# MLA queries as 12 packed tiles with rotary rows placed by DMA and the query norm in the softmax; first loads on a second queue, b heads folded after the transpose, a shorter last token tile

## The chip, the cores and the metric

The kernel runs on one core of a Trainium2 chip. The metric is the device time of one execution in microseconds, and lower is better. The engines are named as in the profile: PE is the matrix engine (TensorE) and PEld its loading of weights, DVE the vector engine, ACT the scalar engine, POOL the GpSimd engine and SP the engine that issues most transfers; SPq and ACTq are the queues of SP and ACT for transfers. All transfers run on the core's 16 DMA engines.

## The reference

Two layers of a streaming encoder are run for a prompt of 256 frames and for eight sample streams of 16 new frames each, which gives 384 columns in all. Layer 0 holds a banded attention ("a", 8 heads) and a differential attention ("b", 4 heads of two maps), layer 1 a multi-head latent attention (MLA, 16 heads). Each mixer stands between two SwiGLU feed-forward blocks, and a final RMSNorm ends the program. What the change touches is this:

```python
def c_project(h, pos, w_in, g_q, g_kv, w_q_up):          # MLA, projections
    cq, ckv, kr = split(h @ w_in, [384, 640])
    q = (rmsnorm(cq, g_q) @ w_q_up).reshape(b, s, 16, 64 + 32)
    q_nope, q_rope = q[..., :64], rope(q[..., 64:], pos)
    ckv = rmsnorm(ckv, g_kv)
    kr = rope(kr, pos)                                    # one rotary key for all heads
def c_attend(q_nope, q_rope, k_nope, v, k_rope, ...):     # MLA, attention
    logits = (q_nope . k_nope + q_rope . k_rope) * 96 ** -0.5
    p = masked_softmax(logits, mask); return p @ v
def rope(x, pos):                                         # x1, x2: the two halves of the 32
    return concat([x1 * cos - x2 * sin, x1 * sin + x2 * cos])
def b_attend(...):                                        # b heads: two maps, one difference
    p = masked_softmax(logits, mask)
    w = p[map 0] - lam * p[map 1]; return w @ v
y = rmsnorm(y, final_norm)                                # the end
```

## The kernel before

**Products.** Activations stand with features on the partitions and the 384 frames along the free axis. Every projection in full precision is made of three products of reduced operands (`mm3`, through `mm`, L94): a weight is split into a high part wh (cast on ACT, L102) and a low part wl (subtraction on DVE, L103), an activation into its own two parts, and high*high, high*low and low*high are summed in PSUM. `load_w` (L105 to L114) issues the transfer of one weight tile `raw` from SP (L109) and makes wh and wl; there are three buffers of each. Small products in plain fp32 (attention, transposes against the identity, column sums) take two passes in the array and show as two records each.

**Order.** The code names the work in one order; the order in which the instructions stand on each engine is set by a scheduling pass over the whole program. An engine runs its own list strictly in that order, and waits where an operand or a buffer isn't there yet. SP's list is the queue of transfers: one that waits holds up all behind it.

**MLA query projection.** `mla_mixer` makes three tiles cq (384 features), two tiles ckv and the rotary key kr; o_ckr (L740) writes kr out, and three ACT copies (L742) repeat its 32 rows down the 128 partitions of kr4. Then the loop over c = 0 to 7 loads one tile of q_up and makes two 128x384 output tiles of nine products each, so 16 tiles and 144 products. A head takes one whole tile of 128 rows: 64 nope rows, 32 rotary rows and the same 32 rows with their halves swapped; the 64 rotary rows meet cos and sin in the tables te and to, and `query` (L776) multiplies each tile by its table, which also carries the query's norm. That norm is brought from columns to all rows by `spread` (L164: three diagonal tiles dg, multiplied by ones). The results are qq: qh for even heads, ql for odd heads. POOL copies the sample columns of the rotary rows to qrs (L778).

**MLA keys.** ke and ko hold the keys of even and odd heads: one half of the partitions from the product of wk and ckv (L807, L808), the other half filled with kr4 by one broadcast transfer each (L798, L799; 64 rows of 8 x 256). The sample queries are multiplied into the latent space by 32 products of wkT and qh or ql (even heads on partitions 0 to 63, odd heads on 64 to 127), which fill qa. Then scores over the cached latents (tiles cb, L853), softmax and values follow, woven with the prompt heads (`soft_prompt`, L372: bias, scale and minimum in one DVE pass; exp on ACT, L374).

**b heads, sample side.** For each of 8 streams the 128 rows of exp hold 4 heads x 2 maps x 16 frames. `turn` (L528) brings them to the key side through `comb_w`, an fp32 product that transposes and adds the two maps at once (L94, T<-comb_w,se); the a heads use a transpose instead (L535). ACT copies the result to pT (L538). `new` does the same for the new frames' weights pn. The PSUM tile T comes from a pool with one buffer, which the transposes of the prompt heads (L401) use too.

**Start and end.** SP issues the gains (L121), then the first eight halves of weights (L966) in turn with the eight tiles of x (L968); until they come, PE runs 14 products of ones. At the end `down_tokens` closes the last feed-forward block token tile by token tile: `half` squares a half on ACT (L279) and multiplies it by the final gains on DVE (L281), `finish` makes the norm from the two sums (L286 to L291) and scales and writes y in two parts (L293 to L296).

Of the kernel before, what the change touches and what calls it, by code (L numbers as in the profile page):

```python
# [11 lines left out]
F32 = mybir.dt.float32  # L12
# [28 lines left out]
C_ID, C_COMB, C_BM, C_M0, C_TE, C_TO = 0, 128, 192, 200, 202, 586  # L41
C_N = 970
# [24 lines left out]
def trunk(ctx, tc, I, O):  # L67
# [56 lines left out]
    comb = con[:, C_COMB:C_COMB + 64]  # L124
    bmask = con[:, C_BM:C_BM + NB]
    rope_e = con[:, C_TE:C_TE + N]
    rope_o = con[:, C_TO:C_TO + N]
# [122 lines left out]
    def down_tokens(fp, gt, down):  # L250
# [26 lines left out]
        def half(t, hf):  # L277
            sq = fp.tile([P, 512], F32, name="fq", bufs=2)
            nc.scalar.activation(sq, ps[t][hf], AF.Square, accum_out=sm[:, t, hf:hf + 1])  # L279
            sl = slice(hf * 512, hf * 512 + 512)  # L280
            nc.vector.tensor_tensor(out=ys[t][:, sl], in0=ps[t][hf], in1=gfin[:, sl], op=ALU.mult)  # L281

        def finish(t):
# [9 lines left out]
            nc.vector.tensor_scalar(y[:, 384:], y[:, 384:], rc, None, op0=ALU.mult)  # L293
            nc.sync.dma_start(out=O["y"][t * P:(t + 1) * P, 384:], in_=y[:, 384:])
            nc.scalar.activation(y[:, :384], y[:, :384], AF.Copy, scale=rc)  # L295
            nc.scalar.dma_start(out=O["y"][t * P:(t + 1) * P, :384], in_=y[:, :384])  # L296
# [69 lines left out]
    def soft_prompt(ap, S, bias, c, bufs=2):  # L366
# [4 lines left out]
        for j, sl, bsl in ((0, slice(0, 128), slice(128, 256)), (1, slice(128, 384), slice(0, 256))):  # L371
            nc.vector.tensor_tensor_reduce(out=s[:, sl], in0=S[:, sl], in1=bias[:, bsl], scale=-c, scalar=BIG,  # L372
# [57 lines left out]
    def even_mixer(sub, g_next):  # L430
        with ExitStack() as es:
# [6 lines left out]
            for nm, nh in (("b", 4), ("a", 8)):  # L438
# [8 lines left out]
            comb_w = mp.tile([P, P], F32, name="comb_w")  # L447
            nc.gpsimd.memset(comb_w, 0.0)
            nc.gpsimd.tensor_copy(out=comb_w.rearrange("p (h w) -> p h w", h=4)[:, :, :NT],
                                  in_=comb.rearrange("p (h t) -> p h t", h=4))  # L450
# [48 lines left out]
            def sample(nm, nout):  # L499
# [6 lines left out]
                rc = ident if nm == "a" else comb_w  # L506
# [22 lines left out]
                def turn(b, e):  # L529
# [4 lines left out]
                    if nm == "a":  # L534
                        nc.tensor.transpose(T[:, :P], e[:, :PAST], ident)  # L535
                    else:
                        mm(T[:, :P], e[:, :PAST], comb_w, True, True)
                    nc.scalar.copy(out=pT, in_=T[:, :P])  # L538
# [17 lines left out]
                def new(hf):  # L556

                    T = ps_t.tile([P, 512], F32, name="T")
                    mm(T[:, :P], pn.rearrange("p b t -> p (b t)"), rc, True, True)
                    pnT = ap.tile([P, P], F32, name="pnT", bufs=1)  # L560
                    nc.scalar.copy(out=pnT, in_=T[:, :P])
# [21 lines left out]
            def b_prompt():  # L583
                q, k, v, _ = qkv["b"]

                def weights(h, _):
                    S = scores_prompt(*[(q[r, h], k[r, h]) for r in (slice(0, 64), slice(64, 128))])
                    (e0, r0), (e1, r1) = [soft_prompt(ap, s, bt["b"][0][:, h], 1.0, 4) for s in S]
# [39 lines left out]
            def a_prompt():  # L628
# [4 lines left out]
                def weights(h, _):  # L633
                    i = h // 2
                    if h % 2 == 0:
                        S[h], S[h + 1] = scores_prompt(*[(q[r, i], k[r, i]) for r in (slice(0, 64), slice(64, 128))])
                    return normed(ap, *soft_prompt(ap, S[h], bt["a"][0][:, h], 1.0, 4))
# [51 lines left out]
    def mla_mixer(sub, g_next):  # L689
        with ExitStack() as es:  # L690
# [43 lines left out]
            nc.vector.tensor_tensor(out=kt, in0=rope_o[0:64], in1=rstd[0:64], op=ALU.mult)  # L734
# [4 lines left out]
            nc.vector.tensor_tensor(out=kr4[0:32], in0=kr4[0:32], in1=krs, op=ALU.add)  # L739
# [3 lines left out]
            nc.gpsimd.tensor_copy(out=kr4s[:, :, PAST:], in_=kr4[:, NP:].rearrange("p (b t) -> p b t", b=NB))  # L743
# [4 lines left out]
            te = slot([P, N], F32, "te", "oh5")  # L748
            to = slot([P, N], F32, "to", "ol5")
            ckl = lambda ct, sl: (cks[ct][0][:, sl], cks[ct][1][:, sl])  # L750

            def norms():

                rq = spread(rcq, 0)[:, :N]
                nc.vector.tensor_tensor(out=te, in0=rope_e, in1=rq, op=ALU.mult)
                nc.vector.tensor_tensor(out=to, in0=rope_o, in1=rq, op=ALU.mult)
# [16 lines left out]
            nc.gpsimd.memset(qrs, 0.0)  # L773

            def query(c, r, ps):
                nc.vector.tensor_tensor(out=qq[r][c], in0=ps[:, :N], in1=(te, to)[r], op=ALU.mult)  # L776
                rp = slice(64 * (1 - r), 64 * (1 - r) + 64)
                nc.gpsimd.tensor_copy(out=qrs[rp, r, :, c], in_=qq[r][c][rp, NP:].rearrange("p (b t) -> p b t", b=NB))  # L778

            held = []  # L780
            for c in range(8):
                w = load_w(I["q_up"][c], 768, cuts=2)
                for r in range(2):
                    ps = ring_tile()
                    for k in range(3):
                        mm3(ps[:, :N], blk(w, 3 * r + k), cqs[k], k == 0, k == 2)
                    held.append((c, r, ps))
                    if (c, r) in ((1, 0), (2, 0), (4, 0)):
                        next(nm)
                    if c:  # L790
                        for a in held:
                            query(*a)
                        held = []
# [56 lines left out]
            def scores():  # L850
                def weights(b, _):
# [14 lines left out]
                    nc.vector.tensor_scalar(mx, mx, -C_SCALE, None, op0=ALU.mult)  # L866
# [61 lines left out]
            def prompt():  # L928
                def weights(h, _):
                    i, r = h // 2, h % 2  # L930
                    S, = scores_prompt((qq[r][i], kk[r][:, i]))
                    return normed(ap, *soft_prompt(ap, S, bmsk, C_SCALE, 3))
# [158 lines left out]
```

## Time and profile before

| what | value |
|---|---|
| median of 3 runs | 1477.79 us (1477.79 to 1477.84) |
| the profiled execution | 1477.37 us, of which the span is 1475.6 us |
| PE busy | 1464.2 us, 99% of the span |
| DVE, ACT, POOL busy | 798.6, 598.3 and 82.6 us |
| granted clock, mean | 0.999 of full speed |
| PE busy in 1054.60 to 1082.50, the query projection | 27.72 of 27.90 us |
| PE busy in 1082.50 to 1102.00, keys and latent queries | 19.05 of 19.50 us |

The span is the time from the first to the last record of the trace; the 1.77 us around it belong to launch and end. A start time in a row is counted from the beginning of the span. Matmuls overlap in the array, so that the duration of a record (0.34 us) is longer than its share of time: the time that a product takes is read from the distance between two starts.

### The profile page before, as it was taken

Reading aid. Unit: us, or ns where it says so; the run is one execution under the profiler, and the core shown is the slowest. Engines: PE = TensorE matmul, PEld = TensorE weight load, DVE = VectorE, ACT = ScalarE, POOL = GpSimd, SP = SyncE. Lnnn points to the kernel's source line nnn. Section 1 sums busy time; section 2 is a strip of 40 time slices with the busy share of each in tenths; the row PEclk is TensorE's granted clock in tenths of the full one; section 3 lists DMA queues with packets and bytes.
Section 4 is the critical chain, followed back from the end, with each engine's and each line's share of the span. In section 5 each row is a group of like instructions: output and inputs, shape, how many; then the busy total and the mean of one; then the engine's idle time right before and its main releaser. Section 6 shows DMA issues by size and latency. Waiting matters only on the chain. (4 is left out here: it accounts for less than half of the span.)

```text
span 1475.6 us, 21816 instructions
## 1 busy us (share of the span) xinstructions
PE 1464.2 (99%) x8683; PEld 1399.7 (95%) x8683; DVE 798.6 (54%) x1456; ACT 598.3 (41%) x1036; POOL 82.6 (6%) x118
## 2 busy tenths in 40 slices
PE   9999999999999999999999999999999999999997
PEld 9999999998778999999999999999997999999886
DVE  7655543357486655553356555443867575555323
ACT  6433333335365433333334333333468453333323
POOL 2000001111001000000100000011110010000000
PEclk9999999999999999999999999999999999999999
DMA  7343344545442343434443333444541243333332
GB/s 242 129 129 127 123 122 119 174 154 169 157 161 97 129 129 129 129 122 118 132 129 128 123 125 125 120 131 143 172 129 44 67 137 128 129 127 124 121 123 78
DMA packets 72501, 191.66 MB, mean 130 GB/s; under 512 B 6704, under 2 KB 27216, under 8 KB 72016
## 3 DMA queue, kind: packets, MB, share of 16 engines
q1 hardware_dynamic: 71968, 189.69, 40.5%
q8 instruction: 68, 1.11, 0.3%
q10 hardware_dynamic: 432, 0.59, 0.1%
q14 instruction: 33, 0.27, 0.1%
HBM read 184.04 MB, written 5.16 MB: 128 GB/s over the span
## 5 line engine op out<-in xcount | busy, mean ns | idle before, releaser
L102 ACT CAST wh<-raw 128x1024 fp32r<-128x1024 f32 (+3 forms) x376 | 340.3, 917 | 762.9 <-issue 288.3
L103 DVE TENSOR_TENSOR wl<-raw,wh 128x1024 fp32r<-128x1024 f32 (+3 forms) x376 | 399.3, 1069 | 287.4 <-ACT wh L102 284.5
L94 PE MATMUL acc<-xh,wh 128*128 128x384 f32 x728 | 245.1, 337 | 0.0
L94 PE MATMUL acc<-xl,wh 128*128 128x384 f32 x728 | 243.4, 334 | 0.0
L94 PE MATMUL acc<-xh,wl 128*128 128x384 f32 x728 | 243.3, 334 | 0.0
L94 PE MATMUL S<-xl,wh 128*128 128x384 f32 x432 | 144.6, 335 | 0.7 <-DVE xl L222 0.7
L94 PE MATMUL S<-xh,wh 128*128 128x384 f32 x432 | 145.0, 336 | 0.0
L94 PE MATMUL S<-xh,wl 128*128 128x384 f32 x432 | 144.3, 334 | 0.0
L94 PEld LDWEIGHTS acc<-xh,wh 128*128 128x128 f32 x728 | 136.2, 187 | 2.5 <-issue 1.9
L94 PEld LDWEIGHTS acc<-xl,wh 128*128 128x128 f32 x728 | 136.3, 187 | 0.9 <-issue 0.2
L94 PEld LDWEIGHTS acc<-xh,wl 128*128 128x128 f32 x728 | 136.2, 187 | 0.3
L184 POOL TENSOR_TENSOR ssq<-ssq,sq 128x384 f32<-128x384 f32 x45 | 53.5, 1189 | 909.7 <-ACT sq L183 899.1
L94 PEld LDWEIGHTS S<-xl,wh 128*128 128x128 f32 x432 | 81.1, 188 | 2.0 <-DVE xl L222 1.7
L94 PEld LDWEIGHTS S<-xh,wh 128*128 128x128 f32 x432 | 81.1, 188 | 0.3
L94 PEld LDWEIGHTS S<-xh,wl 128*128 128x128 f32 x432 | 81.1, 188 | 0.0
L94 PE MATMUL acc<-gl,wh 128*128 128x384 f32 x220 | 74.3, 338 | 0.0
L94 PE MATMUL acc<-gh,wh 128*128 128x384 f32 x220 | 74.3, 338 | 0.0
L94 PE MATMUL acc<-gh,wl 128*128 128x384 f32 x220 | 74.3, 338 | 0.0
L94 PE MATMUL M<-xh,wh 128*128 128x384 f32 x216 | 72.2, 334 | 0.0
L94 PE MATMUL M<-xl,wh 128*128 128x384 f32 x216 | 72.2, 334 | 0.0
L94 PE MATMUL M<-xh,wl 128*128 128x384 f32 x216 | 72.1, 334 | 0.0
L94 PE MATMUL L<-xh,wh 128*128 128x384 f32 x208 | 69.5, 334 | 0.0
(434 smaller groups left out, 2672.9 us busy)
## 6 DMA issues: line engine op xcount, KB each, us to landing
raw<-gu SPq DMA_DIRECT2D x172, 512.0 KB, 3.3
raw<-dn SPq DMA_DIRECT2D x70, 512.0 KB, 3.5
raw<-dn SPq DMA_DIRECT2D x24, 384.0 KB, 3.2
raw<-e_in SPq DMA_DIRECT2D x16, 512.0 KB, 3.5
raw<-e_v SPq DMA_DIRECT2D x8, 512.0 KB, 4.0
raw<-e_out SPq DMA_DIRECT2D x8, 512.0 KB, 3.8
raw<-c_out SPq DMA_DIRECT2D x8, 512.0 KB, 3.3
raw<-q_up SPq DMA_DIRECT2D x8, 384.0 KB, 3.3
```

The source lines that it names most:

```text
L94: nc.tensor.matmul(out, lhsT=l, rhs=r, start=start, stop=stop)
L102: nc.scalar.copy(out=h, in_=src)
L103: (eng or nc.vector).tensor_tensor(out=l, in0=src, in1=h.bitcast(F32), op=ALU.subtract)
L184: nc.gpsimd.tensor_tensor(out=self.acc, in0=self.acc, in1=sq, op=ALU.add)
```

## The change

1. MLA queries. The 16 heads' 32 rotary rows are packed into four tiles of 128 rows, the 64 nope rows into eight: 12 tiles of nine products. The swap of halves moves to the key side: kr4 now holds, per 64 rows, the rotary key and its swapped copy, placed by five transfers instead of three ACT copies, and the cached keys come with swapped rows. The rotary tiles are multiplied by cos and by sin (`rotary`, into the tiles turned0 and turned1, which use the memory of ke and ko), and `place` carries them to their heads' rows in qq by 32 transfers of 32 x 384 numbers (48 KB) inside the core's memory. The nope tiles are copied to qq by ACT, 16 copies of 64 x 384. The query's norm isn't multiplied in any more: it goes as a scale per row into the softmax (ncq for the prompt, csq for the samples; csq comes from one product of 128 x 8), and `spread` stays for the keys alone.
2. b heads. comb_w is gone: the weights are transposed as for the a heads, and `both_maps` adds the two maps with two DVE operations, from PSUM to pT (ten times: eight streams and two halves of new frames). The a heads' two products for pn become transposes as well.
3. Start. The gains and the first two tiles of x are issued from ACT's queue.
4. End. The second half of the last token tile isn't multiplied by the gains by itself; one DVE operation multiplies it by gains and norm from PSUM. ACT comes first, and the two parts are cut at 512 instead of 384.

```diff
-    nc.sync.dma_start(out=gains, in_=I["gains"])
+    nc.scalar.dma_start(out=gains, in_=I["gains"])
...
-            nc.sync.dma_start(out=xd, in_=I["xT"][:, d])
+            (nc.scalar if d < 2 else nc.sync).dma_start(out=xd, in_=I["xT"][:, d])
...
-            nc.vector.tensor_tensor(out=ys[t][:, sl], in0=ps[t][hf], in1=gfin[:, sl], op=ALU.mult)
+            if t < TT - 1 or hf < HF - 1:
+                nc.vector.tensor_tensor(out=ys[t][:, sl], in0=ps[t][hf], in1=gfin[:, sl], op=ALU.mult)
...
+                nc.vector.scalar_tensor_tensor(y[:, cut:], ps[t][1], rc, gfin[:, cut:], op0=ALU.mult, op1=ALU.mult)
...
+            def both_maps(out, T):
+                m = [T[:, :P].rearrange("p (h m t) -> p h m t", h=4, m=2)[:, :, i:i + 1].to_broadcast([P, 4, 2, NT])
+                     for i in range(2)]
+                nc.vector.tensor_copy(out=out.rearrange("p (h m t) -> p h m t", h=4, m=2), in_=m[0])
+                nc.vector.tensor_tensor(out=out.rearrange("p (h m t) -> p h m t", h=4, m=2),
+                                        in0=out.rearrange("p (h m t) -> p h m t", h=4, m=2), in1=m[1], op=ALU.add)
...
-                        mm(T[:, :P], e[:, :PAST], comb_w, True, True)
-                    nc.scalar.copy(out=pT, in_=T[:, :P])
+                    nc.tensor.transpose(T[:, :P], e[:, :PAST], ident)
+                    settle(pT, T)
...
+            for at in (32, 96):
+                nc.sync.dma_start(out=kr4[at:at + 16], in_=kr4[16:32])
+                nc.sync.dma_start(out=kr4[at + 16:at + 32], in_=kr4[0:16])
+            nc.sync.dma_start(out=kr4[64:96], in_=kr4[0:32])
             nc.sync.dma_start(out=O["ckr"], in_=kr4[0:32])
-            for j in range(1, 4):
-                nc.scalar.copy(out=kr4[32 * j:32 * j + 32], in_=kr4[0:32])
...
+            def rotary(c, w):
+                for j in range(2):
+                    ps = up(w, j)
+                    for t, tab in enumerate((rcos, rsin)):
+                        nc.vector.tensor_tensor(out=turned[c][:, j, t], in0=ps[:, :N], in1=tab, op=ALU.mult)
+            def place(c):
+                for j in range(2):
+                    for q in range(4):
+                        h = 8 * c + 4 * j + q
+                        r = h % 2
+                        for t in range(2):
+                            at = 64 * (1 - r) + 32 * t
+                            nc.sync.dma_start(out=qq[r][h // 2][at:at + 32], in_=turned[c][32 * q:32 * q + 32, j, t])
+            w = load_w(I["q_rope"][0], 768, cuts=2)
+            w1 = load_w(I["q_rope"][1], 768, cuts=2)
+            rotary(0, w)
+            w = load_w(I["q_nope"][0], 768, cuts=2)
+            rotary(1, w1)
+            place(0)
+            next(nm)
+            for c in range(4):
+                w1 = load_w(I["q_nope"][c + 1], 768, cuts=2) if c < 3 else None
+                if c == 0:
+                    place(1)
+                for j in range(2):
+                    ps = up(w, j)
+                    for r in range(2):
+                        rr = slice(64 * r, 64 * r + 64)
+                        nc.scalar.copy(out=qq[r][2 * c + j][rr], in_=ps[rr, :N])
...
                     for r in range(2):
                         nc.scalar.activation(e[:, r], S[:, r * NK:(r + 1) * NK], AF.Exp, bias=mx[:, r:r + 1],
-                                             scale=C_SCALE, accum_out=sm[:, r:r + 1])
+                                             scale=csq[:, 0, b:b + 1], accum_out=sm[:, r:r + 1])
```

How the change moves instructions is shown at three places. The first is SP's queue in the query projection. Before, from the rotary key's write-out to the first loads for the output projection, it holds:

```order
L740 DMA o_ckr<-kr_9792 32x384
L799 DMA ko<-kr_9792 64x8x256
L109 DMA raw<-q_up 128x768 x2
L798 DMA ke<-kr_9792 64x8x256
L109 DMA raw<-q_up 128x768
L109 DMA raw<-wk 128x1024 x2
L766 DMA o_ckv<-ckv 128x2x384
L109 DMA raw<-c_out 128x1024 x6
```

After the change the same stretch holds 16 rows of placing (L812), two transfers each, of which the last three stand here:

```order
L753 DMA o_ckr<-kr_9800 32x384
L812 DMA qh_9832<-turned_9850 32x384 x2
...
L812 DMA ql_9846<-turned_9851 32x384 x2
L812 DMA qh_9839<-turned_9851 32x384 x2
L812 DMA ql_9847<-turned_9851 32x384 x2
L783 DMA o_ckv<-ckv 128x2x384
L109 DMA raw<-q_nope 128x768
L842 DMA ke<-kr_9800 64x8x256
L843 DMA ko<-kr_9800 64x8x256
L109 DMA raw<-wk 128x1024 x2
```

The fourth load of q_nope, the two key broadcasts and the loads of wk now stand behind 32 placings, with five transfers for kr4 ahead of o_ckr, and both broadcasts stand directly ahead of wk.

The second place is PE's list where the sample queries meet wkT. Before, even heads (qh) and odd heads (ql) alternate, after the value products, 31 of them in one row:

```order
L94 MATMUL acc<-wh,ckvl_9690 128x512
L94 MATMUL M<-ql_9831,wkT 128x128
L94 MATMUL S<-qh_9824,wkT 128x128
L94 MATMUL M<-ql_9832,wkT 128x128
L94 MATMUL S<-qh_9825,wkT 128x128
L94 MATMUL M<-ql_9833,wkT 128x128
```

After the change they stand in groups of one kind at three places: twelve ahead of the seventh nope tile, eight behind the last, twelve after the value products. The first group is this:

```order
L94 MATMUL S<-cqh_9688,wl 128x384
L94 MATMUL S<-qh_9832,wkT 128x128
L94 MATMUL S<-qh_9833,wkT 128x128
L94 MATMUL S<-qh_9834,wkT 128x128
L94 MATMUL S<-qh_9835,wkT 128x128
L94 MATMUL L<-qh_9836,wkT 128x128
L94 MATMUL L<-qh_9837,wkT 128x128
...
L94 MATMUL S<-ql_9844,wkT 128x128
L94 MATMUL S<-ql_9845,wkT 128x128
L94 MATMUL M<-cqh_9639,wh 128x384
```

Products of even and odd heads, which stood side by side in pairs, now mostly follow products of their own kind; the row M<-cqh begins the seventh nope tile, which needs the fourth load of q_nope.

The third place is PE's list in the b heads, where the turn of pn is followed by the next turn of se; both go into T, and the rows between are an input projection. Before:

```order
L94 MATMUL acc<-xh_1903,wh 128x384
L94 MATMUL T<-comb_w,pn 128x128
L94 MATMUL acc<-xl_1904,wh 128x384
L94 MATMUL acc<-xh_1903,wl 128x384
L94 MATMUL acc<-xh_1994,wh 128x384
L94 MATMUL T<-comb_w,se 128x128
```

After:

```order
L94 MATMUL acc<-xh_1903,wh 128x384
L566 MATMUL T<-con,pn 128x128
L94 MATMUL acc<-xl_1904,wh 128x384
L94 MATMUL acc<-xh_1903,wl 128x384
L94 MATMUL acc<-xh_1994,wh 128x384
L94 MATMUL acc<-xl_1995,wh 128x384
L94 MATMUL acc<-xh_1994,wl 128x384
L94 MATMUL acc<-xh_2087,wh 128x384
L544 MATMUL T<-con,se 128x128
```

Six products instead of three now lie between the two users of T.

## Rows read from the trace of the kernel before

**Rows 1.** page, part 1, TensorE: busy us (share) x instructions
```profile
PE 1464.2 (99%) x8683; PEld 1399.7 (95%) x8683; DVE 798.6 (54%) x1456; ACT 598.3 (41%) x1036; POOL 82.6 (6%) x118
```

**Rows 2.** timeline of PE, MLA query tiles: start us, us, engine, line, operation, output<-inputs
```profile
1054.60 0.42 PE L94 MATMUL L<-cqh,wh 128*128 128x384 f32 x1
...
1056.26 0.34 PE L94 MATMUL acc<-cqh,wh 128*128 128x384 f32 x1
...
1057.84 0.34 PE L94 MATMUL S<-cqh,wh 128*128 128x384 f32 x1
...
1059.95 0.34 PE L94 MATMUL M<-cqh,wh 128*128 128x384 f32 x1
...
1061.16 0.42 PE L94 MATMUL M<-cql,wh 128*128 128x384 f32 x1
...
1082.53 0.28 PE L94 MATMUL acc<-ckvh,wh 128*128 128x256 f32 x1
```

**Rows 3.** timeline of PE, the products with wkT, to the first cb
```profile
1097.95 0.37 PE L94 MATMUL M<-ql,wkT 64*128 64x128 f32 x1
...
1098.27 0.27 PE L94 MATMUL M<-ql,wkT 64*128 64x128 f32 x1
1098.28 0.27 PE L94 MATMUL S<-qh,wkT 64*128 64x128 f32 x1
...
1101.71 0.51 PE L94 MATMUL acc<-cb,qa 128*128 128x144 f32 x2
```

**Rows 4.** timeline of SP, the issuing of transfers: start us, us to issue
```profile
1.66 0.50 SPq L968 DMA_DIRECT2D x<-xT  x1
2.20 0.43 SPq L966 DMA_DIRECT2D raw<-gu  x1
...
1056.38 0.36 SPq L740 DMA_DIRECT2D o_ckr<-kr  x1
```

**Rows 5.** DMA issues of 1050 to 1090: count, KB each, median us to landing
```profile
raw<-q_up SPq DMA_DIRECT2D x5, 384.0 KB, 3.3
...
raw<-wk SPq DMA_DIRECT2D x2, 512.0 KB, 4.3
ko<-kr SPq DMA_DIRECT2D x1, 512.0 KB, 5.4
```

**Rows 6.** timeline of ACT, the cast of the second wk load
```profile
1079.43 1.05 ACT L102 CAST wh<-raw 128x1024 fp32r<-128x1024 f32 x1 [2.11 <-PE acc L94]
```

**Rows 7.** timeline of PE, a turn of b weights, then one of a
```profile
355.67 0.49 PE L94 MATMUL T<-comb_w,se 128*128 128x128 f32 x2
356.09 0.45 PE L94 MATMUL L<-kb,qbd_b 128*32 128x144 f32 x8
...
424.48 0.33 PE L535 MATMUL T<-con,se 128*128 128x128 f32 x1 [0.33 <-ACT wT L403]
424.74 0.45 PE L94 MATMUL L<-kb,qbd_a 128*32 128x144 f32 x8
```

**Rows 8.** instructions on tile pT, 340 to 385: ns min/median/max
```profile
L538 ACT COPY pT<-T x6: 239/258/266, 348.8 to 384.0; 128x128 f32<-128x128 f32 x6
```

**Rows 9.** timeline of DVE, one pass over 128x128 numbers
```profile
353.04 0.28 DVE L526 TENSOR_SCALAR se<-se,ssm 128x128 f32<-128x128 f32 x1
```

**Rows 10.** waits of PE over the whole span: us in total, times, longest
```profile
PE S L94 <- DVE xl L222: 0.7, 3, 0.4
```

**Rows 11.** timeline of DVE, the end of the last token tile
```profile
1468.50 0.69 DVE L281 TENSOR_TENSOR y<-S,gfin 128x512 f32<-128x512 f32 x1
...
1469.17 0.21 DVE L286 TENSOR_SCALAR fc<-fs 128x1 f32<-128x1 f32 x1
```

**Rows 12.** windows at the end: us, PE busy (instructions), granted clock, DMA share, GB/s
```profile
1466.00:1468.00 2.00, 1.74 (x8) 1.00 0.46 180
1468.00:1471.00 3.00, 0.00 (x0) 1.00 0.24 90
1471.00:1472.00 1.00, 0.00 (x0) 0.60 0.99 377
```

More of the change, by code (lines that the diff above doesn't have):

```diff
@@ L40 @@
 G_N = 54
[L41 to L42 removed]
+C_ID, C_SEL, C_BM, C_M0, C_TE, C_TO = 0, 128, 144, 152, 154, 538
+C_N = 922
 def weave(*parts):
@@ L505, in sample @@
                 at_b = lambda b: slice((b % 4) * P, (b % 4) * P + P)
-                rc = ident if nm == "a" else comb_w
+                settle = both_maps if nm == "b" else lambda out, T: nc.scalar.copy(out=out, in_=T[:, :P])
                 def weights(b, _):
@@ L773, in mla_mixer @@
             nc.gpsimd.memset(qrs, 0.0)
-            def query(c, r, ps):
-                nc.vector.tensor_tensor(out=qq[r][c], in0=ps[:, :N], in1=(te, to)[r], op=ALU.mult)
-                rp = slice(64 * (1 - r), 64 * (1 - r) + 64)
[L778 to L793, printed above, removed]
+            turned = [mp.tile([P, 2, 2, N], F32, name=f"turned{i}", tag=t) for i, t in enumerate(("ke", "ko"))]
@@ new lines, in up @@
+            def up(w, j):
+                ps = ring_tile()
+                for k in range(3):
+                    mm3(ps[:, :N], blk(w, 3 * j + k), cqs[k], k == 0, k == 2)
+                return ps
+            def rotary(c, w):
[11 more added lines that the diff above has]
+                            nc.sync.dma_start(out=qq[r][h // 2][at:at + 32], in_=turned[c][32 * q:32 * q + 32, j, t])
@@ new lines, in mla_mixer @@
+            w = load_w(I["q_rope"][0], 768, cuts=2)
[14 more added lines that the diff above has]
+                        nc.scalar.copy(out=qq[r][2 * c + j][rr], in_=ps[rr, :N])
+                if c < 2:
+                    next(nm)
+                w = w1
@@ L796, in mla_mixer @@
+            for r in range(2):
+                rp = slice(64 * (1 - r), 64 * (1 - r) + 64)
+                for c in range(8):
+                    nc.gpsimd.tensor_copy(out=qrs[rp, r, :, c], in_=qq[r][c][rp, NP:].rearrange("p (b t) -> p b t", b=NB))
+            nc.gpsimd.tensor_copy(out=kr4s[:, :, PAST:], in_=kr4[:, NP:].rearrange("p (b t) -> p b t", b=NB))
             ke = mp.tile([P, 8, NP], F32, name="ke")
@@ L1032, in _host @@
     o["c_kr"] = f(np.concatenate([kr, kr[:, :, 16:], kr[:, :, :16]], 2).transpose(1, 0, 2)).reshape(P, KT * 64)
-    q = A["c_w_q_up"][0].reshape(3, P, 8, 2, 96)
-    nope, r = q[..., :64], q[..., 64:]
-    s = np.concatenate([r[..., 16:], r[..., :16]], -1)
-    ev = np.concatenate([nope, r, s], -1)[:, :, :, 0]
-    od = np.concatenate([r, s, nope], -1)[:, :, :, 1]
-    o["q_up"] = f(np.stack([ev, od], 3).transpose(2, 1, 3, 0, 4)).reshape(8, P, 768)
+    q = A["c_w_q_up"][0].reshape(3, P, 16, 96)
+    for nm, w in (("q_rope", q[..., 64:]), ("q_nope", q[..., :64])):
+        w = w.reshape(3, P, -1, 2, P)
+        o[nm] = f(w.transpose(2, 1, 3, 0, 4)).reshape(-1, P, 768)
     kv = A["c_w_kv_up"][0].reshape(2, P, 16, 2, 64)
```

78 lines of the change are left out of this document (39 added, 39 removed).

## The prediction

> **What bounds the kernel now.** I read the page's shares first, because they say where an edit can count at all: PE is busy for 1464.2 us of the span of 1475.6 us [rows 1]. So an edit is worth what it takes from PE's list, less what PE must newly wait for. The second view is PE's timeline in the stage with the largest edit. In the MLA query projection one output tile follows the next after 1057.84 - 1056.26 = 1.58 us [rows 2], which is 0.1755 us for each of its nine products. The stage runs from 1054.60 to 1082.53, that is 27.93 us, of which 16 tiles are 25.3 us; the other 2.65 us are column sums and two spreads of a norm. The third view is SP's timeline with the landing times of its transfers, because the change puts 38 small transfers into a queue that also feeds the weights. Before, the loads of this stage come early enough that PE has next to no wait there: the one wait of note in the view is that on the diagonal tile of the spread, which is inside the 1061.16 - 1059.95 = 1.21 us between two products that otherwise start 0.1755 us apart [rows 2].
>
> **The change part by part, MLA.** Four tiles fall away: 4 x 1.58 = 6.3 us less on PE. The spread of the query's norm cost 1.21 - 0.18 = 1.0 us [rows 2]; one product of 8 columns takes its place, and I leave 0.4 us for it and its operand, so -0.6 us. The extra DVE and ACT work (eight multiplications by sin, 16 copies) lies on engines that are busy for about half of the span [rows 1], beside PE's products, and I cost it at nothing; if that cover were gone, a tile's buffer would come free late, by a copy's time each.
>
> The latent queries become dearer. Before, a product of an even head and one of an odd head start 0.01 us apart [rows 3]: they lie on different halves of the partitions and go side by side. The 31 products that stand together before make 15 pairs and one, and take 1101.71 - 1097.95 = 3.76 us [rows 3], some 0.22 us a turn; with the 32nd, which stands elsewhere, 4.0 us. After the change neighbours are mostly of one kind, and I count 11 + 6 + 11 = 28 turns in the three groups, 6.2 us. That is +2.2 us.
>
> Then the queue. SP can't place anything before the rotary key is ready, which is when o_ckr is issued, 1056.38 [rows 4]. From there it issues five transfers for kr4, o_ckr and 32 placings, 38 in all, and after them o_ckv and the fourth load of q_nope. The issue of o_ckr, a transfer of the same 32 x 384 shape, took 0.36 us; in the busy queue at the start a tile of x took 2.20 - 1.66 = 0.54 us to the next [rows 4]. These are my bounds for one placing, and between them I take the middle, 0.45 us, as the placings follow one another without a break but are small. So the queue is through at 1056.38 + 38 x 0.45 = 1073.5, o_ckv makes it 1073.9, the load lands 3.3 us later [rows 5], and its first half must be cast: 0.5 us, from 1.05 us for 1024 columns [rows 6] at 384. PE can start the seventh nope tile at 1077.7. When would PE want it? Ahead of it stand ten tiles (15.8 us), the 2.65 us of other work less the 0.6 us saved, and the first group of 11 turns (2.4 us): 1054.60 + 15.8 + 2.05 + 2.4 = 1074.9. PE waits about 2.8 us.
>
> The loads of wk come next. The two key broadcasts stand directly ahead of them, 512 KB each; ko took 5.4 us to land before [rows 5]. ke goes out at about 1074.4, wk at 1075.6. If the broadcasts don't slow it, wk lands after its own 4.3 us [rows 5], at 1079.9; if the three go one after the other, after 5.4 + 5.4 + 4.3 us from ke's issue, at 1089.5. I take the middle, 1084.7, and with the cast of 1.05 us [rows 6] 1085.7. PE comes there after two tiles and six turns, 1077.7 + 3.2 + 1.3 = 1082.2, and waits 3.5 us. Before, the broadcasts went out between the loads of q_up, and wk found them gone. The sum for MLA: -6.3 - 0.6 + 2.2 + 2.8 + 3.5 = +1.6 us. Two score products of the first prompt heads move ahead into this stage as well; that moves work and removes none.
>
> One rule of the Trainium skill speaks against the middle term. What the row shows is 0.36 us of issue for a transfer of 48 KB [rows 4], and 38 of them make 14 to 21 us. The page "DMA: Bandwidth & Descriptors" (Issuing engines are not separate DMA queues) holds that the time in which a sequencer initiates a transfer is usually small relative to the transfer itself, so that one wouldn't look for a stall there. By that rule the wait of 2.8 us would be nothing and the whole sum 2.8 us lower; by the row the issue is the term that decides, and I keep it.
>
> **b heads.** A turn of b weights takes 356.09 - 355.67 = 0.42 us of PE, a transposition in the a heads 424.74 - 424.48 = 0.26 us [rows 7]. Twelve become the latter (eight turns, two for pn in b, two in a): -1.9 us. Against it, T is left by two DVE passes instead of one copy. The copy took 0.26 us [rows 8], a pass of DVE over 128x128 numbers 0.28 us [rows 9], so a turned tile comes 0.3 us later at the least, and T, which has one buffer, is held as long; in the order other DVE work of the softmax stands between the two passes. Ten times 0.3 us would be +3.0, none is hidden then; the order puts six products instead of three between one user of T and the next at the place shown, which hides it. I take four of ten late, +1.2, and so -0.7 us, with -1.9 and +1.1 as ends.
>
> **Start.** SP's first weights go out ahead of the gains and two tiles of x. PE's waits on the first activations are 0.7 us in all [rows 10], and no more can be won there; the cost could be ACT, which now issues three transfers of up to 0.54 us [rows 4] before its first cast. I take -0.4 us, between -0.7 and +0.5.
>
> **End.** The DVE product by the gains starts at 1468.50 and holds the sum for the last norm up to 1469.17 [rows 11]. It goes, 0.67 us; the last scaling is a little longer on both engines (512 columns instead of 384 on ACT, from PSUM on DVE). I take -0.5 us, between -0.7 and 0.
>
> The sum is +1.6 - 0.7 - 0.4 - 0.5 = 0.0 us on the profiled execution of 1477.37 us (span 1475.6 us and 1.77 us around it). The median of the runs stands 0.42 us above it, and the prediction goes from the median: 1477.8 us.
>
> **Rivals.**
> - The waits are hidden: a placing is issued in 0.36 us and wk lands after its own 4.3 us. Then the queue is through 3.4 us earlier, the seventh nope tile's weights are there at 1074.3, before PE wants them, and those of wk at 1077.5, where PE wants them at 1079.4. Both waits are gone. It is 2.8 + 3.5 = 6.3 us less: 1471.5 us. For it speaks o_ckr's own row; against it that a transfer issued behind another took longer at the start.
> - The queue is slower: 0.54 us for each placing, as for a tile of x. It adds 38 x 0.09 = 3.4 us to the wait for q_nope, and all behind moves with it: 1481.2 us. It decides from about 0.53 us on. Against it: those tiles have 128 rows, these 32.
> - The clock falls. After its last product PE stood still from 1467.74 (1.74 us busy of the window from 1466), the granted clock was 1.00 up to 1471.0, and 0.60 on average in the microsecond after that, on the way to the lower level of 1.2 GHz [rows 12]. A stop of 3.5 us ahead of wk is about as long. If PE then works at half speed for as long as it had stood, 3.5 us, it loses 1.8 us: 1479.6; if for all of the key and value products (1082.53 to 1097.95), 15 us: 1493. The page "TensorE: Matmul & The Clock Gate" (HAM oscillation) describes this for kernels that wait on transfers between groups of products. No row of this trace shows PE at work at the lower level.
> - Every turn in the b heads waits: T held by DVE for its two passes and the work between them, about 0.9 us a turn instead of 0.3: ten make +9 - 1.9 instead of -0.7, 1485.6 us at the worst, half of it 1481.
>
> **How the numbers follow.** I give the forecast 0.50, the hidden waits 0.24, the slow queue 0.14, the clock 0.08 and the b heads 0.04. About 0.2%, 2.96 us, is what a measurement of this kernel can tell from no change: faster is under 1474.83, slower over 1480.75. Faster holds most of the hidden waits (0.21) and an edge of the forecast (0.04), 0.25. Slower holds the slow queue (0.12), half of the clock's case, most of the b heads and an edge of the forecast (0.05), 0.24. The rest, 0.51, is no change. The forecast's own range is 1474.8 to 1480.6, from the ends of the small terms and placings between 0.40 and 0.50 us. With the rivals on both sides it becomes 1472.0 to 1481.8.
>
> **What would show it.** On SP, 38 short issues in a row from about 1056 on, at 0.45 us each, and the fourth q_nope load at about 1074; two waits of PE on the casts of raw, of about 3 us each, one ahead of the seventh nope tile and one ahead of the first product of wk; latent queries that start 0.22 us apart; transposes in the b heads of 0.26 us with few waits on DVE for T; the last norm's sum right after the last square. The prediction is wrong if the loads of q_nope and wk arrive before PE wants them, if a placing takes over 0.5 us, or if the granted clock is under 1 in the key stage.

## The result, and the profile after

The changed kernel takes 1490.13 us (median of 4 runs, 1488.86 to 1492.20) against 1477.79 us before: the ratio is 1.0088, with a 95% interval from 1.0077 to 1.0100. It is slower by 12.3 us, outside the predicted range. The profiled execution took 1488.86 us, its span is 1487.1 us.

PE's waits over the whole span come first, since PE's list got shorter (in us in total, times, longest):

```profile
PE M L94 <- ACT wh L102: 13.0, 1, 13.0
PE acc L94 <- POOL ones L129: 1.0, 1, 1.0
PE acc L94 <- ACT wh L102: 0.9, 1, 0.9
```

One wait of 13.0 us for a cast of weights is longer than the whole loss. PE's timeline shows where it stands, ahead of the seventh nope tile, and that what follows is slow as well:

```profile
1073.01 0.27 PE L94 MATMUL S<-ql,wkT 64*128 64x128 f32 x1
1086.28 0.69 PE L94 MATMUL M<-cqh,wh 128*128 128x384 f32 x1 [13.00 <-ACT wh L102]
...
1089.32 0.52 PE L94 MATMUL acc<-cqh,wh 128*128 128x384 f32 x1
```

The tile that begins at 1086.28 takes 1089.32 - 1086.28 = 3.04 us, where one took 1.58 us [rows 2]. The granted clock says why (window, length, PE busy and products, granted clock, DMA share, GB/s):

```profile
1072.00:1076.00 4.00, 1.28 (x15) 1.00 0.34 80
1076.00:1077.00 1.00, 0.00 (x0) 0.63 0.26 62
1077.00:1086.00 9.00, 0.00 (x0) 0.50 0.65 170
1086.00:1089.00 3.00, 2.72 (x8) 0.50 1.16 202
1089.00:1090.00 1.00, 1.00 (x5) 0.54 1.22 230
1090.00:1094.00 4.00, 3.06 (x24) 1.00 0.92 355
```

PE began its last product before the stop at 1073.01. The clock was 1.00 up to 1076, fell in the microsecond after that to 0.50, which is the lower level of 1.2 GHz, and was back at 1.00 by 1090, with PE at work again from 1086.28 on. That is the fall that [rows 12] showed at the end of the kernel before, now with work behind it. It cost 1.5 us on this tile and some 0.3 us on the next.

PE waits for ACT's cast of the fourth q_nope load, and ACT for the transfer. ACT's timeline:

```profile
1085.71 0.92 ACT L102 CAST wh<-raw 128x384 fp32r<-128x384 f32 x2 [11.92 <-DMA raw<-q_nope]
```

SP's timeline shows why the transfer is late (start, us to issue, x2 for two in a row; of the placings the first, the longest and the last row stand):

```profile
1055.48 0.61 SPq L750 DMA_DIRECT2D kr<-kr  x1
...
1058.70 0.58 SPq L753 DMA_DIRECT2D o_ckr<-kr  x1
1059.71 1.15 SPq L812 DMA_DIRECT2D qh<-turned  x2
...
1063.44 2.06 SPq L812 DMA_DIRECT2D ql<-turned  x2
...
1079.50 1.23 SPq L812 DMA_DIRECT2D ql<-turned  x2
1080.83 0.53 SPq L783 DMA_DIRECT2D o_ckv<-ckv  x1
1081.45 0.41 SPq L109 DMA_DIRECT2D raw<-q_nope  x1
...
1083.45 3.92 SPq L109 DMA_DIRECT2D raw<-wk  x2
```

The five transfers for kr4 and o_ckr take 0.58 to 0.63 us of issue each. The 32 placings run from 1059.71 to 1080.83, 0.66 us each on average: two of them in a row take 1.15 to 1.23 us, one pair 2.06 us. Only then come o_ckv and the load of q_nope, at 1081.45, 7.5 us later than I had worked out. Of the rows that answer to [rows 4], o_ckr itself takes 0.58 us here instead of 0.36.

The stages, from PE's first products in each (starts read from the timelines of both kernels):

| stretch | before | after | difference |
|---|---|---|---|
| first real product (S<-xh) | 6.94 | 5.79 | -1.15 |
| from there to the query projection | 1047.66 | 1047.33 | -0.33 |
| query projection, to the first product with ckv | 27.93 | 40.89 | +12.96 |
| keys, values, latent queries, to the first cb | 19.18 | 19.43 | +0.25 |
| attention, to the output projection | 53.62 | 54.39 | +0.77 |
| output projection and last block, to PE's last product | 312.02 | 312.14 | +0.12 |
| from there to the end | 8.24 | 7.13 | -1.11 |

The query projection holds the loss. Its own account: four tiles less -6.3, the spread replaced -0.6, the first two groups of latent queries now in this stage +4.0, the waits +13.0 and +0.9, the low clock +1.8, in sum +12.8 of the 12.96 us. The +0.77 us of the attention are no finding: in the profiles of the kernels with the new MLA part below, this stretch takes between 53.3 and 55.4 us.

The other parts did what they were meant to. A turn of b weights is now a transposition of 354.80 - 354.54 = 0.26 us, as the a heads' in [rows 7], and it stands as one record (x1), where the product with comb_w had two; the text ahead, which counts the transposes among the products with two records, is wrong there:

```profile
354.54 0.33 PE L544 MATMUL T<-con,se 128*128 128x128 f32 x1
354.80 0.45 PE L94 MATMUL L<-kb,qbd_b 128*32 128x144 f32 x8
```

And at the end the sum for the last norm starts (L287, 1481.13) 0.23 us after ACT began to read it out, where 0.67 us of DVE work stood between before [rows 11]. Timeline of the end, all engines:

```profile
1480.90 0.19 ACT L279 ACTIVATION_READ_ACCUMULATOR fq<-acc 128x1 f32 x1
1481.13 0.21 DVE L287 TENSOR_SCALAR fc<-fs 128x1 f32<-128x1 f32 x1
```

### The profile page after: what moved, and what is told of

The parts are those of the page before. It is cut to its first block, busy times and chain, and to the rows that moved or that the text cites. A ratio compares the mean times of both kernels' runs of the same rounds, so it can differ in the third digit from the quotient of the medians.

```text
span 1487.1 us, 21771 instructions
## 1 busy us (share of the span) xinstructions
PE 1462.9 (98%) x8631; PEld 1394.3 (94%) x8631; DVE 798.0 (54%) x1463; ACT 602.2 (40%) x1035; POOL 79.1 (5%) x117
## 3 DMA queue, kind: packets, MB, share of 16 engines
q8 instruction: 68, 1.11, 0.3%
## 4 chain that ended last, share of the span: by engine, by line
PE 96%; ACT 1%; DMA 1%; issue 1%; SPq 1%; DVE 0%; ACTq 0%; POOL 0%; POOLq 0%; DVEq 0%
PE acc L94 44%; PE S L94 24%; PE L L94 13%; PE M L94 13%; PE T L407 1%; DMA raw<-gu 1%; SPq L812 0%; ACT wh L102 0%; PE T L94 0%; DMA raw<-q_nope 0%; DMA cb<-cckvT 0%; PE T L544 0%; ACT ko L852 0%; DVE wl L103 0%; ACT ke L851 0%
## 5 line engine op out<-in xcount | busy, mean ns | idle before, releaser
L184 POOL TENSOR_TENSOR ssq<-ssq,sq 128x384 f32<-128x384 f32 x45 | 53.6, 1191 | 909.2 <-ACT sq L183 898.5
```

Source lines behind the costliest of these rows:

```text
L184: nc.gpsimd.tensor_tensor(out=self.acc, in0=self.acc, in1=sq, op=ALU.add)
```

## The experiments

All are changes of one of the two kernels; every ratio is to the kernel before on the same chip, with a 95% interval.

**The small parts alone (e1_rest).** The kernel before with the start, the b heads and the end of the change:

```diff
-    nc.sync.dma_start(out=gains, in_=I["gains"])
+    nc.scalar.dma_start(out=gains, in_=I["gains"])
...
-                        mm(T[:, :P], e[:, :PAST], comb_w, True, True)
-                    nc.scalar.copy(out=pT, in_=T[:, :P])
+                    nc.tensor.transpose(T[:, :P], e[:, :PAST], ident)
+                    settle(pT, T)
...
```

> The kernel before with the three small parts only (first loads on ACT's queue, b heads folded after a transpose, shorter last token tile); the MLA part stays as before. Theory A: the whole loss stands in the MLA query stage, because 38 small transfers hold SP's queue ahead of a weight load. Then the stage takes 27.9 us again, no PE wait is over 1 us, and the three parts give about -1.2 (b heads) and -1.1 (end) us, with the start somewhere between 0 and -1: 1474.5 to 1476 us. Rival B: part of the loss comes from the small parts, hidden by luck of the start: then the time is 1478 us or more. Side question: the down products took 0.1766 us instead of 0.1760 us after the change; if that comes with the smaller table of constants of the MLA part, it is 0.1760 us again here.

Measured: 1475.38 us, ratio 0.9987 (0.9978 to 0.9996), that is -1.9 us. The query projection takes 27.93 us again (1053.52 to 1081.45). Theory A holds: the loss is in the MLA part, and the small parts are a small gain.

**The placings later in the queue (e2_late).** The changed kernel with the calls moved:

```diff
-            place(0)
             next(nm)
...
-                if c == 0:
-                    place(1)
...
+            wks = [load_w(I["wk"][c]) for c in range(2)]
+            place(0)
+            place(1)
             ke = mp.tile([P, 8, NP], F32, name="ke")
...
-                w = load_w(I["wk"][c])
+                w = wks[c]
```

> The changed kernel with only the places in the code moved at which placing is asked for: behind the fourth q_nope load and the two loads of wk; same transfers, same count. Theory A (a load stands behind the placings in one queue): the 13.0 us wait of PE goes to under 2 us, the granted clock stays at 1.00 in the stage, a placing still takes 0.6 to 0.66 us of SP, the queue is through at about 1083, and the time falls by 12 to 15 us to 1475 to 1478 us. Rival B (the placings themselves slow the other transfers down while both are in flight): the loads take clearly longer to land than 3.3 us and PE still waits several us, 1482 us or more. Rival C (the key broadcasts, now the last in the queue, take the place of the late load): PE waits 3 us or more for ke or ko in the attention, about 1480 us.

Measured: 1479.52 us, ratio 1.0015 (1.0006 to 1.0024), 10.6 us less than the changed kernel. The fourth load of q_nope now goes out ahead of the placings, at 1060.50, and PE's 13 us wait is gone. SP's timeline:

```profile
1060.50 0.36 SPq L109 DMA_DIRECT2D raw<-q_nope  x1
```

The load landed 3.2 us after its issue with the placings in flight behind it, so rival B falls. But not all came back, since two new waits of PE appeared, and the clock was low around them:

```profile
PE acc L94 <- ACT ko L852: 3.4, 1, 3.4
PE acc L94 <- ACT ql L826: 1.2, 1, 1.2
```

```profile
1074.00:1080.00 6.00, 4.81 (x37) 1.00 0.32 74
1080.00:1084.00 4.00, 3.78 (x29) 0.57 0.36 83
1084.00:1088.00 4.00, 0.84 (x4) 0.87 0.51 107
```

Rival C had the right place and the wrong reason. ACT's timeline shows that its copy to ko waited for a placing of ql, not for a broadcast of the key:

```profile
1086.74 0.91 ACT L852 COPY ko<-acc 64x256 f32<-64x256 f32 x3 [3.75 <-DMA ql<-turned]
```

turned1 lies in ko's memory. Until the last placing has read it (issued up to 1085), ACT may not write ko, the product's PSUM tile stays taken, and PE stops.

**The same with other memory for the rotary tiles (e5_late_room).**

```diff
-            turned = [mp.tile([P, 2, 2, N], F32, name=f"turned{i}", tag=t) for i, t in enumerate(("ke", "ko"))]
+            turned = [mp.tile([P, 2, 2, N], F32, name=f"turned{i}", tag=t) for i, t in enumerate(("qa", "vv"))]
...
-            vv = mp.tile([P, 2, 1024], F32, name="vv")
+            vv = mp.tile([P, 2, 1024], F32, name="vv", tag="vv")
```

> The kernel of e2_late, with the tiles turned0 and turned1 in other memory: in that of qa and vv, which are written later than ke and ko. Theory A: what was left in e2_late, PE's wait of 3.4 us for ACT's copy to ko and of 1.2 us for a copy to ql, came from ko's memory, which holds turned1 until the last placing has read it (1085 us) and so holds ACT's copies, PSUM and PE; the clock fell in that wait. With other memory no wait over 1 us is left, the clock stays at 1.00 and the time is 4.6 us of waits and some 1.5 us of clock less: 1472.5 to 1475 us. Rival C: the two key broadcasts, issued only after the last placing at about 1085, land too late for the first prompt heads, and PE waits 2 us or more for S<-ke: 1476 us or more.

Measured: 1475.87 us, ratio 0.9990 (0.9981 to 0.9999). No wait of PE in the key stage is over 1 us any more, and the clock is whole (0.999 over the span). What is left of the two waits of e2_late is 0.5 us for ko and 0.9 us for ql:

```profile
PE acc L94 <- ACT ql L826: 0.9, 1, 0.9
PE acc L94 <- ACT ko L852: 0.5, 1, 0.5
```

So the wait for ko came from the memory. That the clock fell in that wait, as expected here, isn't what e2_late shows: its windows have 0.57 in 1080 to 1084, and PE began to wait at 1083.78.

From the query projection to the first cb it is 44.2 us instead of 47.1 before and 60.3 after the change. So without the late load the MLA part is a gain, of 2.9 us in this stretch. The time itself, some 1 us above the theory's range, is no better than that of the small parts alone: the attention took 55.4 us instead of 53.6 in the profiled execution, with single waits of under 1 us, and the stretch from the first real product to the query projection, which this edit doesn't touch, took 1049.0 us instead of 1047.7.

**No placing transfers (e3_direct).** DVE writes each head's rows to their place, 32 multiplications of 32x384 instead of eight of 128x384:

```diff
+                        for q in range(4):
+                            h, rq = 8 * c + 4 * j + q, slice(32 * q, 32 * q + 32)
+                            at = 64 * (1 - h % 2) + 32 * t
+                            nc.vector.tensor_tensor(out=qq[h % 2][h // 2][at:at + 32], in0=ps[rq, :N], in1=tab[rq], op=ALU.mult)
```

> The changed kernel without any placing transfer: DVE writes each head's 32 rotary rows straight to their place, 32 multiplications of 32x384 (0.55 us each, 17.6 us) instead of 8 of 128x384 (4.4 us). Theory A: the wait of 13.0 us is gone and the queue of SP is free; 13 us more of DVE in a stage of some 25 us are either hidden, 1474 to 1477 us, or make PE wait a little for a free PSUM tile, up to 1479. Rival B (lost pairs, reordered latent queries and other PE work make the loss): the time stays over 1485 us.

Measured: 1486.55 us, ratio 1.0063 (1.0051 to 1.0076). The cure is nearly as bad as the trouble. PE now waits for DVE:

```profile
PE acc L94 <- DVE wl L103: 5.1, 1, 5.1
PE M L94 <- DVE ql L807: 3.2, 1, 3.2
```

DVE was busy for 28.7 of the 30 us from 1050 to 1080, the low halves of the weights waited behind them, and the clock fell to 0.50 here too. The time alone would fit rival B as well; the waits name DVE. My expectation had counted DVE's total against the stage, and not that its instructions stand in line ahead of the casts that PE waits for.

**The placings on ACT's queue (e4_place_act).**

```diff
-                            nc.sync.dma_start(out=qq[r][h // 2][at:at + 32], in_=turned[c][32 * q:32 * q + 32, j, t])
+                            nc.scalar.dma_start(out=qq[r][h // 2][at:at + 32], in_=turned[c][32 * q:32 * q + 32, j, t])
```

> The changed kernel with the 32 placings issued from ACT's queue instead of SP's. Theory A, narrow (only SP's queue matters): the load of q_nope goes out early, PE's wait is under 2 us, 1475 to 1478 us. Theory A with a price (whoever issues is held for 0.6 us each): ACT, which must also cast each weight and copy the nope rows, is held for about 20 us, and PE waits for casts instead, some 5 to 13 us: 1480 to 1490 us, with the wait of PE named on an ACT cast although the raw weights have long landed. Rival B (the transfers in flight, not their issue, are the trouble): no change from 1490 us, and the raw loads land late.

Measured: 1488.33 us, ratio 1.0075 (1.0063 to 1.0088). The second form of theory A: who issues is held. ACT's timeline (its queue as ACTq), and PE's wait:

```profile
1080.26 1.24 ACTq L812 DMA_DIRECT2D ql<-turned  x2
1081.54 0.47 ACT L829 COPY qh<-acc 64x384 f32<-64x384 f32 x1 [12.79 <-DMA qh<-turned]
```

```profile
PE acc L94 <- ACT wh L102: 12.9, 2, 9.3
```

Two placings take mostly 1.24 us on ACT as well, at the most 2.34. The casts and copies stand behind them, while the load that they are for had gone out at 1061.0.

**The placings on GpSimd's queue (e6_place_pool).**

```diff
-                            nc.sync.dma_start(out=qq[r][h // 2][at:at + 32], in_=turned[c][32 * q:32 * q + 32, j, t])
+                            nc.gpsimd.dma_start(out=qq[r][h // 2][at:at + 32], in_=turned[c][32 * q:32 * q + 32, j, t])
```

> The changed kernel with the 32 placings issued from GpSimd's queue; everything else as it was. GpSimd has 7 us of other work in the stage. Theory A: SP's queue is free, the fourth q_nope load and the loads of wk go out when their buffers are free, PE's 13 us wait is gone: 1475 to 1479 us if GpSimd issues a placing in 1 us or less (32 us, through at about 1090), with a wait for ko's memory as in e2_late. If one takes 2 us, the latent queries of the rotary rows and ko come at about 1120 and PE waits over 15 us: over 1490 us. Rival B: transfers in flight slow the loads: raw tiles land clearly later than 3.5 us.

Measured: 1476.15 us, ratio 0.9996 (0.9987 to 1.0005), 14 us less than the changed kernel. GpSimd's timeline:

```profile
1074.90 0.98 POOL L812 DMA_DIRECT2D ql<-turned  x2
```

A placing takes 0.49 us there, with stops between some, so that all 32, from 1056.4 to 1075.9, take 19.5 us instead of the 21.1 us on SP. So the chain is hardly shorter; what has changed is that no weights stand behind it. The two loads of wk took 5.5 and 6.8 us to land, where the median before is 4.3 [rows 5]: loads do land later there, as rival B had it, but PE waits for none of them. What is left is a low clock in the key stage, around waits of 1.0 and 1.1 us for ACT's copies to ko and ql:

```profile
1074.00:1080.00 6.00, 4.85 (x33) 0.91 0.97 253
1080.00:1084.00 4.00, 3.02 (x16) 0.50 0.58 174
1084.00:1088.00 4.00, 4.00 (x26) 0.78 0.56 107
```

**The dose (e7_place_split).** Each placing cut into two of 192 columns, 64 transfers with the same bytes:

```diff
+                            for s in (slice(0, 192), slice(192, 384)):
+                                nc.sync.dma_start(out=qq[r][h // 2][at:at + 32, s], in_=turned[c][32 * q:32 * q + 32, j, t, s])
```

> The changed kernel with each placing cut into two of half the columns: 64 transfers of 32 x 192, the same bytes. If the time is that of issuing (per transfer), SP is held 32 times 0.62 us longer, some 20 us, PE's wait goes from 13 to about 33 us and the time to 1510 us. If it goes by bytes, an issue takes some 0.3 us and nothing changes: 1490 us.

Measured: 1512.16 us (one run). PE's wait:

```profile
PE M L94 <- ACT wh L102: 32.9, 1, 32.9
```

From 13.0 to 32.9 us, 19.9 us more for 32 more transfers: 0.62 us each, though each carries half the bytes. The expectation of 33 us and 1510 us was met: here the price goes by the transfer and not by its bytes.

**Both remedies together (e9_pool_room)**: GpSimd's queue, and the memory of qa and vv, in the changed kernel's order.

```diff
+                            nc.gpsimd.dma_start(out=qq[r][h // 2][at:at + 32], in_=turned[c][32 * q:32 * q + 32, j, t])
...
+            turned = [mp.tile([P, 2, 2, N], F32, name=f"turned{i}", tag=t) for i, t in enumerate(("qa", "vv"))]
...
```

> Both remedies together: the 32 placings issued from GpSimd's queue (0.5 us each in e6_place_pool, through at 1076) and turned0 and turned1 in the memory of qa and vv. Theory: in e6_place_pool what was left of the loss were waits for ko's memory with a fall of the clock (0.50 in 1080 to 1084, 0.78 after that); in e5_late_room these waits were gone and the key stage took 23.0 us instead of 26.0. Together: granted clock 1.00 throughout, query and key stages some 43 to 44 us instead of 47.1 before, and 1472.5 to 1474.5 us, faster than the kernel before and than the small parts alone (1475.4). Rival: other work fills the gap, so that it stays at 1475.5 to 1476.5 as in e5_late_room.

Measured: 1473.54 us, ratio 0.9972 (0.9962 to 0.9982), -4.0 us. From the query projection to the first cb it is 44.3 us, and the clock stays whole (two windows of this stretch):

```profile
1054.80:1076.00 21.20, 20.79 (x125) 1.00 0.87 220
1076.00:1099.10 23.10, 20.15 (x149) 1.00 0.46 145
```

PE's waits for ACT's copies are no shorter than in e6_place_pool, where they were 1.1 us for ql and 1.0 us for ko:

```profile
PE acc L94 <- ACT ql L829: 1.3, 1, 1.3
PE acc L94 <- ACT ko L852: 0.9, 2, 0.5
```

So the theory came out in its time and not in its mechanism: with the other memory the fall of the clock is gone and the key stage is 2.9 us shorter (23.1 us instead of 26.0), but the waits that it was put down to are still there. The clock goes with the time from run to run as well: in the ten runs of e6_place_pool its mean lies between 0.999 (1474.74 us) and 0.995 (1478.25 us), in the nine of this kernel it is 0.998 or 0.999. Why it stays up here isn't shown.

This version beats the kernel before and the changed one. Against the small parts alone (0.9978 to 0.9996) the intervals touch, and the two weren't run side by side; the gain over them is likely and not shown.

**Where the tiles lie (e8_pad, e10_pool_room_8).** Two runs asked about a small loss outside the MLA part: a down product of the feed-forward blocks takes 0.1767 us to the next after the change, 0.1760 before and in e1_rest (means over 1581 of them), so 1.1 us. The table of constants is smaller after the change, and later tiles lie elsewhere in SBUF.

```diff
-C_N = 922
+C_N = 954
```

> The changed kernel with 32 unused columns in the table of constants, which moves every later tile in SBUF by 128 bytes; the work is the same. Theory of place: the step of the down products (0.1760 us before and in e1_rest, 0.1767 us with the smaller table) depends on where the tiles lie, and is another number than 0.1767 here, 0.1760 or a third value. Rival: it comes with something else of the MLA change and stays 0.1767.

Measured: 0.1767 us, 1491.99 us (one run). The tiles moved and the step didn't.

The second run is the kernel of e9_pool_room with another width:

```diff
-C_N = 922
+C_N = 930
```

> The kernel of e9_pool_room with eight unused columns in the table of constants, so that all later tiles lie 32 bytes further on in SBUF. In e8_pad 128 bytes didn't change the step of the down products (0.1767 us). In the kernel before and in e1_rest, where it is 0.1760, the gh tiles start 32 bytes off a multiple of 64; after the change and in e8_pad they start on one. Theory of place, second form: what counts is that offset, and the step is 0.1760 us here, for 1.1 us less over 1581 products. Rival: it isn't the place and the step stays 0.1767, the time that of e9.

Measured: 0.1767 us again; 1472.40 us, ratio 0.9967 (0.9955 to 0.9980), the same as e9 within the intervals. Both forms of that theory fell, and what makes the step stays open. A third form, the distance between the two operands, wasn't tried.

## Why the prediction was wrong

- **The step that failed** is the one on the price of a placing: "These are my bounds for one placing, and between them I take the middle, 0.45 us". It measured 0.66 us, above the upper bound of 0.54 too, and the queue was through at 1080.8 instead of 1073.5. As the load then went out 7.5 us later, PE came 1.6 us earlier than worked out and the load landed in 4.2 us instead of 3.3, the wait was 13.0 us instead of 2.8. The mechanism was named, as a term of the sum and as the slow-queue rival; the size was wrong.
- **Why the bounds were wrong.** I took the nearest rows by shape: o_ckr, of 32 x 384, and a tile of x. Both go from or to HBM. The trace of the kernel before held two transfers inside SBUF, as the placings are, the key broadcasts:

```profile
1056.92 0.66 SPq L799 DMA_DIRECT2D ko<-kr  x1
...
1060.81 0.63 SPq L798 DMA_DIRECT2D ke<-kr  x1
```

  They take 0.66 and 0.63 us to issue. I had put that down to their 512 KB. The changed kernel has transfers inside SBUF of 24, 48 and 512 KB, on 16, 32 and 64 rows, and each holds SP for 0.6 to 0.7 us, but for the one long pair; e7_place_split shows the same for half the columns. The kind isn't all: o_ckr, which took 0.36 us with the queue free, takes 0.58 us right behind the five transfers for kr4, while the first of these took 0.61 us with nothing just ahead of it. With 0.64 us from these rows the sum would have been 38 x 0.19 = 7.2 us higher, 1485.0 us, and the forecast would have been "slower", still 5.1 us short.
- **The clock** was held apart as a rival at 0.08, though it isn't independent: the long wait brought it here. It cost 1.8 us on two tiles here. That the rival's lower price was 1.8 us as well is luck: it was worked out for a stop of 3.5 us and for half speed as long as the stop, while the stop was 13.0 us and the clock was back within the second tile. The Trainium skill, "TensorE: Matmul & The Clock Gate" (HAM oscillation), describes such a fall in a wait on transfers; the granted clock above agrees for this stop.
- **The rule weighed against the queue**, that issuing is usually small beside the transfer ("DMA: Bandwidth & Descriptors" of the Trainium skill, Issuing engines are not separate DMA queues), did not help here: 0.6 us of issue stands beside 1.9 us to landing. That the issuing sequencer's time is what another queue saves, as the same section says, is what e6_place_pool shows: SP no longer issues the placings, and the kernel takes 14 us less.
- **wk** was predicted at 3.5 us of wait and measured 0.9. Its weights came about as worked out: ACT begins their cast 6.6 us after the seventh tile begins, where I had 7.0:

```profile
1092.90 2.00 ACT L102 CAST wh<-raw 128x1024 fp32r<-128x1024 f32 x2
```

  PE came later: for two tiles and eight latent queries it took from 1086.28 to 1093.07, 6.8 us instead of 4.5, of which the low clock made 1.8. So the low clock stands here largely in the place of a wait for wk that would have been some 2.7 us (an estimate, 0.9 + 1.8), and by this estimate it adds little to the loss.
- **Latent queries** without their partners: predicted +2.2 us. The three groups take 2.4, 1.6 and 2.5 us, 6.5 in all, against 4.0: +2.5 us, right.
- **b heads**: predicted -0.7 us. From the first product with kb to the output projection of layer 0 it is 103.68 us before (337.23 to 440.91), 103.08 in e1_rest and 103.13 after the change, -0.6 us: right.
- **Start**: predicted -0.4 us. The first real product stands at 5.79 us instead of 6.94, but that is the time of the products of ones ahead of it, which varies from run to run (last section). The first product with kb, before the other parts of the change begin, starts at 337.23 before and between 336.2 and 338.2 us in the kernels with the new start; no gain is shown.
- **End**: predicted -0.5 us, measured -1.1 after the change and -0.7 in e1_rest (8.24 to 7.53 us from PE's last product).

## What to carry to other kernels

Price a new transfer by the rows of its own kind, from where to where it goes, before its shape or its bytes, and multiply by all that stands ahead of the next thing that the queue must do: a cheap transfer in a weight queue costs what the weights behind it cost. When such a chain is found, move it to a queue that carries no weights, on an engine that has no casts to do, and look at once for the memory that it keeps (here ko's in e2_late), since that can be the next wait. After a long wait, look at the clock too (0.50 after the 13.0 us here), and ask whether the time lost at it would have been waited elsewhere.

## What the runs showed of the hardware that I had not expected

- Issuing a transfer inside SBUF takes 0.6 to 0.7 us on SP, the same for 16, 32 and 64 rows and for 192 and 384 columns, mostly 0.62 us on ACT, and 0.49 us on GpSimd. A load of q_nope from HBM takes 0.33 to 0.41 us on SP, but the two loads of wk behind the key broadcasts take 3.92 us together, so what stands ahead of a transfer counts as well.
- In e2_late and e6_place_pool the granted clock fell to about half (0.57 and 0.50 in 1080 to 1084) while PE was busy for 3.78 and 3.02 of these 4 us, with latent queries on half of the rows, and without a wait of over 1.2 us before it. In e9_pool_room it stayed at 1.00.
- The products of ones at the start run at two speeds, 0.213 and 0.111 us from one record to the next, and where the speed changes differs between the profiled executions. PE's timeline, of the kernel before and then of the changed one:

```profile
0.99 6.19 PE L94 MATMUL acc<-ones 128*128 128x128 f32 x28 [0.99 <-POOL ones L129]
```

```profile
0.99 5.04 PE L94 MATMUL acc<-ones 128*128 128x128 f32 x28 [0.99 <-POOL ones L129]
```

  The same 28 records take 6.19 us in the one and 5.04 us in the other, though the profile gives the clock as 1.00 there in both. In the runs above, the first real product stands between 5.79 and 6.99 us. It doesn't move the whole program: e6_place_pool has the latest first product (6.99) and the changed kernel the earliest (5.79), and both come to the first product with kb at 336.2 us.
